# Second MLP of a two-block layer: h two tiles a strip, tables without GpSimd products, a bank for the row broadcast

## The chip, the cores and the metric

The kernel runs on one core of one Trainium2 chip, as one launch. The metric is the device time of a run in microseconds. A core has five engines with an instruction queue each: TensorE (PE, matrix products; its weight loads are shown as PEld), VectorE (DVE), ScalarE (ACT), GpSimd (POOL) and SyncE (SP), which here issues the weight transfers. An engine takes its queue in order. Products are written to eight banks of PSUM, from which VectorE and ScalarE read; everything else lies in SBUF.

## The reference, cut to what matters

The first block has two layers, each a mixer and then an MLP with modulated normalisation. The second block, which follows, has among other branches a state space one (S5).

```python
for l in range(2):
    ...                                            # mixer, x = x + g_m * rmsnorm(y)
    h = rmsnorm(x, norm_g[l, 2]) * (1.0 + sc_f) + sh_f
    y = jnp.square(jax.nn.relu(h @ w_up[l])) @ w_down[l]
    x = x + g_f * rmsnorm(y, norm_g[l, 3])
...                                                # second block: h @ w_in, then branches
```

There are 256 tokens, a width of 1024 and 4096 hidden units, all in fp32. The state space branch needs tables that depend on its parameters alone: powers 0 to 8 of a complex number lambda for 32 groups, times the input and output matrices B and C. As real numbers an entry is X1 times the real part plus X2 times the imaginary part: two products and one sum.

## The kernel before, in words

**Splitting.** Every fp32 weight and activation is written as a high part (fp32r) and the rest (low part), and a product is three matmuls: high by high, low by high, high by low. For each weight unit of 128 x 1024, ScalarE writes the high part (whi, line 379) and VectorE the rest (wlo, line 382). Three buffers each hold whi and wlo. The units stream in through SP into six buffers of two units.

**The MLP** (`mlp`, line 1283) walks over 32 strips of 128 hidden units. A strip is an up product (24 matmuls of 128x256) from h into a bank, then squared Relu, then a split into ml_h and ml_l (`act`), then an outer product with a unit of w_down (`kouter`, 24 matmuls) that adds into four banks `acc` of two output tiles each. `kouter` of strip j-1 is written behind `act` of strip j.

The first six strips don't wait for h. `begin` computes them from x and the modulation alone, with the scale per token (rs) still missing, into banks with the tags q, q, d, d, q, q. `act` of these strips reads the bank on VectorE with a product by rs (the tile ml_v), adds a column and applies Relu on ScalarE (ml_r), squares on VectorE (`stt`), and splits. The four banks of `acc` have the tag q as well, so they are those of the strips 0, 1, 4 and 5, each free when its strip's ml_v was read out.

**h** is made by `hprep(k, ...)` for eight tiles of 128 x 256: VectorE scales into a temporary t, ScalarE adds the shift into xh, VectorE writes the rest xl. All eight are written in the code behind strip 4, and t is a tile of the tag ml_v with two buffers, which `act` uses too. Strip 6 is the first that reads h.

**The tables** (`s5_prep`) are made during the second layer's MLP. It is a generator; the loop over strips advances it from strip 5 to strip 23 in proportion to the weights `_S5W` of its steps. It loads on ScalarE's queue, computes powers and angles in small VectorE steps, then nine table tiles WC (128 x 512: a VectorE product, a GpSimd product into s5tm, a VectorE sum) and 32 tiles WBs (128 x 128, the same three steps), which TensorE transposes in groups. GpSimd's queue also issues the transfers of the tables to memory and back (s5kd, s5TP).

**The end of the MLP** (`postnorm`, `plainsplit`): the four banks are squared and summed, the scale of each token is broadcast by TensorE into a bank (`rowsof`, tag o in a pool px of one bank), VectorE multiplies by it and adds to x in four steps (`xstep`), and x is split into xh, xl. Then the pool px closes and the pool pa opens with seven banks, and the branch's first product (`tokmajor`, 128x512, from xh and xl) is written there.

**Order.** The order of the instructions of each engine is not the one of the code: a planner goes through the program with estimated costs, and gives each free engine the ready instruction that stands first in the code. Only instructions inside `inorder` blocks keep the order of the code. The result is a fixed queue for each engine. Buffers and banks of one tag are given out in turn, with a wait for the last reader.

Of the kernel before, what the change touches and what calls it, by code (L numbers as in the profile page):

```python
# [28 lines left out]
AF = mybir.ActivationFunctionType  # L29
OP = mybir.AluOpType  # L30
# [4 lines left out]
P = 128  # L35
T = 256
# [6 lines left out]
_S5W = [0.1, 2, 1.5, 2.5, 2.5, 1.1, 2.6, 2.6, 1.5, 1.5, 1.1, 2, 2.5, 2.2] + [1.2] * 9 + [0.6] * 4 + \  # L43
# [268 lines left out]
class Prog:  # L312
# [967 lines left out]
        return self.postnorm(pool, xT, acc, l, 1, n, ("up", l, 1), ("up", l, 2))  # L1280


    def mlp(self, l, xT, pre, fill, n=0, up=None, yB=None):

        with self.pool(f"mlp{l}") as pool, self.psum(f"pf{l}", d=2, q=4, o=2):
            w = self.sb(up or pool, [P, 4608], "s5WC", F32R)[:, :16 * (T + 2)]
            w = w.rearrange("p (a k t) -> p a k t", a=2, k=8)
            ps, rs, hprep = self.begin(xT, pre, l, 2, (w[:, 0], w[:, 1]), pre[1],
                                       [("up", l, s) for s in range(6)], "qqddqq")
            del w  # L1290
            X = [self.sb(self.xp, [P, 8, T], k, F32R) for k in ("xh", "xl")]
            acc = None
            pend = []
            work = nst = 0

            def act(j):
                r = self.sb(pool, [P, T], "ml_r", bufs=2)
                if j < 6:
                    v = self.sb(pool, [P, T], "ml_v", bufs=2)
                    p, c = ps[j]  # L1300
                    self.tt(v, p[:, 0:T], rs, OP.mult)
                    self.act(r, v, AF.Relu, bias=c)
                    self.stt(r, v, c, r, OP.add, OP.mult)
                    ps[j] = p = None
                else:
                    p = self.strip(("up", l, j), X) if j < 31 else lastp
                    self.act(r, p, AF.Relu)
                    if l and j < 32:
                        self.act(r, r, AF.Square)
                    else:  # L1310
                        self.stt(r, p, 0.0, r, OP.max, OP.mult)
                hh = self.sb(pool, [P, T], "ml_h", F32R, 3)
                hl = self.sb(pool, [P, T], "ml_l", F32R, 3)
                self.hl(hh, hl, r)
                pend.append((hh, hl))

            raw = lambda j: self.unit(("down", l, j), 1024)
            for j in range(31):
                act(j)
                if j == 1:  # L1320
                    acc = [self.pt([P, 2, T], "q") for _ in range(4)]
                if j == 4:
                    for k in range(8):
                        hprep(k, X[0][:, k], X[1][:, k], self.sb(pool, [P, T], "ml_v", bufs=2))
                    del hprep
                    self.adasum()
                if j:
                    self.kouter(acc, raw(j - 1), *pend.pop(0), j == 1, False)

                while l and 5 <= j < 24 and work < sum(_S5W) * (j - 4) / 19 - 0.01:  # L1330
                    work += _S5W[nst]
                    nst += 1
                    next(fill, None)
                if not l:
                    next(fill, None)
            for _ in fill:
                assert False
            self.adasum()
            lastp = self.strip(("up", l, 31), X)
            W = self.split(raw(30), 1024)  # L1340
            W2 = self.split(raw(31), 1024)
            act(31)
            self.koutermm(acc, W, *pend.pop(0), False, False)
            W = None
            if not l:
                self.presplit(("in", 1, "cq", 0))
                self.presplit2(("in", 1, "cq", 0))
            self.koutermm(acc, W2, *pend.pop(0), False, True)
            W2 = None
            X = None  # L1350
            if l:
                return self.postnorm(pool, xT, acc, l, 3, n, yB=yB())
            return self.postnorm(pool, xT, acc, l, 3, n, ("in", 1, "cq", 1), ("in", 1, "ckv", 0))
# [39 lines left out]
    def s5_prep(self, pool, sx, dp):  # L1393

        nc = self.nc
# [28 lines left out]
        Lr, Li = sb([P, 9, 32], "s5Lr"), sb([P, 9, 32], "s5Li")  # L1424
# [15 lines left out]
        f = lambda a: a.rearrange("p a b -> p (a b)")  # L1440
# [35 lines left out]
        bc = lambda a: a[:, :, None].to_broadcast([P, 32, 16])  # L1476
# [3 lines left out]
        X1, X2, tm = sb([P, 32, 16], "s5X1"), sb([P, 32, 16], "s5X2"), sb([P, 32, 16], "s5tm", bufs=2)  # L1480
# [5 lines left out]
        tm = sb([P, 32, 16], "s5tm", bufs=2)  # L1486
        self.tt(tm, C1, bc(ci), OP.mult)
        self.tt(X2, X2, tm, OP.subtract)
        B2 = v3(rb[:, 512:1024])
# [3 lines left out]
        for k in range(9):  # L1493
            w = WC[:, :, k]
            tm = sb([P, 32, 16], "s5tm", bufs=2)
            self.tt(w, X1, bc(Lr[:, k]), OP.mult)
            nc.gpsimd.tensor_tensor(tm, X2, bc(Li[:, k]), op=OP.mult)
            self.tt(w, w, tm, OP.add)
            yield

# [17 lines left out]
        for q in range(4):  # L1518
            gs = slice(8 * q, 8 * q + 8)
            b8 = lambda a: a[:, gs, None].to_broadcast([P, 8, 16])  # L1520
            WBs = sb([P, 8, 8, 16], "s5WBs")
            for s in range(8):
                w = WBs[:, :, s]
                tm = sb([P, 8, 16], "s5tm", bufs=2)
                self.tt(w, B1[:, gs], b8(Lr[:, s]), OP.mult)
                nc.gpsimd.tensor_tensor(tm, B2[:, gs], b8(Li[:, s]), op=OP.mult)
                self.tt(w, w, tm, OP.add)
                if s % 4 == 3:
                    yield
            for g in range(0, 8, 4):  # L1530
                ps = self.pt([P, 4, P], "o")
                for a in range(4):
                    self.tr(ps[:, a], WBs[:, g + a].rearrange("p s h -> p (s h)"))
                self.act(self.WB[:, 8 * q + g:8 * q + g + 4], ps)
                yield
# [971 lines left out]
    def run(self, out):  # L2507
        tc, nc, pool = self.tc, self.nc, self.pool
        with tc.tile_pool(name="dram", bufs=1, space=DRAM) as dp:
# [3 lines left out]
            with pool("ring") as self.ring, pool("wp") as self.wp:  # L2513
                xT = self.start1(c1.enter_context(pool("l01", "left")))
                c0 = ExitStack()
                self.l01b = c0.enter_context(pool("l01b", "left"))
                with pool("rp") as q:
                    self.rope(q)
                self.i8 = self.sb(self.l01b, [P, 8], "i8", F32R)
                self.act(self.i8, self.C("i8"))  # L2520
                for l in range(2):
                    self.mixconst(l)
                with self.psum("p0", d=2, o=1):
                    self.adas(1)
                    self.y0 = self.xsums(xT)
                    self.adas(1)
                    for k in (("cq", 0), ("cq", 1), ("ckv", 0)):
                        self.presplit(("in", 0) + k)
                pre = self.mixer(0, xT, [None, None, None], (1, 0, 1, 1), 1)
                pre = self.mlp(0, xT, pre, self.filler(2, 12), 1)  # L2530
                pre = self.mixer(1, xT, pre, (1, 0, 0, 1), 1)
                c0.close()
                with pool("s5t") as s5t:
                    with pool("s5x") as sx:
                        half = lambda: [self.sb(sx, [P, 4, T], k) for k in ("s5rb", "s5rc")]
                        pre = self.mlp(1, xT, pre, self.s5_prep(s5t, sx, dp), up=s5t, yB=half)
                        with self.psum("px", o=1):
                            X = self.plainsplit(xT, pre)
                    pre = self.y0 = None
                    xd = dp.tile([P, 8 * T], F32, name="xd")  # L2540
                    nc.gpsimd.dma_start(xd, xT.rearrange("p a b -> p (a b)"))
                    c1.close()
                    thp = c1.enter_context(pool("thp", "left"))
                    self.hgb = self.sb(thp, [P, 24], "hgb")
                    self.ts(self.hgb, self.col("gate_b"), 0.5, None, OP.mult)
                    self.th = [self.sb(thp, [P, 8, T], f"th{i}") for i in range(2)]
                    G = [self.sb(thp, [P, 4, T], k, F32R) for k in ("gh", "gl")]
                    with pool("s5") as p, self.psum("pa", d=3, x=4):
                        self.bg = chain(self.gates(X, 1), self.gates(X, 0, 0, 6))
                        self.s5(p, dp, X, G)  # L2550
                self.pos = -(-self.pos // CH) * CH
            self.nraw, self.nw = 3, 2
            with pool("ring") as self.ring, pool("wp") as self.wp:
# [106 lines left out]
```

## Time and profile before

| | |
|---|---|
| runs | 1461.97 us median of 3 (1461.76 to 1469.58) |
| profiled execution | 1464.17 us, its span 1462.4 us |
| mean granted TensorE clock | 0.979 of full |
| TensorE busy | 1369.8 us (94%) |
| VectorE busy | 868.5 us (59%) |
| ScalarE busy | 649.4 us (44%) |
| GpSimd busy | 81.4 us (6%) |
| moved by DMA | 311.71 MB, 213 GB/s in the mean |

Busy time counts an instruction from its start to its end; instructions of one engine overlap a little at their ends. "Idle before" and "waited for" name the instruction whose end let a waiting one go. The granted clock of TensorE has two levels, 1.0 (2.4 GHz) and half; a value between them is the mean over a stretch. In the trace the first layer's MLP lies at about 194 to 400 us and the second layer's at about 566 to 782; the first branch product comes at 790.

### The profile page before, as it was taken

The page shows a single profiled execution, that of the slowest core. Times are in us where ns is not written, and L with a number is a line of the kernel's source. Part 1 is how long each engine was busy: PE and PEld are TensorE (multiplying, and loading weights), DVE is VectorE, ACT ScalarE, POOL GpSimd, SP SyncE. Part 2 cuts the span into 40 slices and gives each one's busy share as a digit, 9 for nine tenths or more (in the row PEclk, how much of TensorE's full clock was granted, in tenths as well). Part 3 has the DMA queues.
Part 4 walks back from the last instruction along what each step waited for, and adds up shares of the span by engine and source line. Part 5 has one row for each costly group of instructions (what it writes and reads, how often), then busy time and mean ns, then how long its engine had stood idle before and what let it go on. Part 6 is the DMA issues. An engine that isn't in the chain of part 4 may idle for free. (4 is left out here: it accounts for less than half of the span.)

```text
span 1462.4 us, 26516 instructions
## 1 busy us (share of the span) xinstructions
PE 1369.8 (94%) x10795; PEld 1124.7 (77%) x10795; DVE 868.5 (59%) x1983; ACT 649.4 (44%) x1295; POOL 81.4 (6%) x128
## 2 busy tenths in 40 slices
PE   4999999999999999899998989999998999999996
PEld 1787788999988878898997978888987864445442
DVE  2776677555588667998565465567746663222224
ACT  2655555444556545564555444355242432121121
POOL 0000000000000010023220010000000013000001
PEclk9999999999999999999999999999999999999998
DMA  9735467665565247444783333232124969999980
GB/s 371 295 140 202 186 247 278 224 252 198 178 259 197 89 176 268 156 159 171 186 233 115 116 104 143 89 145 87 59 92 159 405 218 366 420 410 375 399 327 30
DMA packets 45999, 311.71 MB, mean 213 GB/s; under 512 B 5296, under 2 KB 5744, under 8 KB 9648
## 3 DMA queue, kind: packets, MB, share of 16 engines
q1 hardware_dynamic: 41264, 293.10, 52.9%
q0 software_dynamic: 3312, 13.50, 3.5%
q10 hardware_dynamic: 1296, 3.36, 0.6%
q8 instruction: 87, 1.43, 0.4%
q14 instruction: 40, 0.33, 0.1%
HBM read 306.46 MB, written 3.47 MB: 212 GB/s over the span
## 5 line engine op out<-in xcount | busy, mean ns | idle before, releaser
L382 DVE TENSOR_TENSOR wlo<-raw,whi 128x1024 fp32r<-128x1024 f32 (+3 forms) x292 | 332.2, 1141 | 196.2 <-ACT whi L379 190.7
L379 ACT ACTIVATE whi<-raw 128x1024 fp32r<-128x1024 f32 (+3 forms) x292 | 284.5, 978 | 282.4 <-PE ps_d L393 202.4
L393 PE MATMUL ps_d<-xh,whi 128*128 128x256 f32 (+1 forms) x1072 | 310.8, 291 | 1.6 <-ACT whi L379 0.9
L393 PE MATMUL ps_d<-xh,wlo 128*128 128x256 f32 x816 | 234.3, 287 | 3.7 <-DVE wlo L382 3.6
L393 PE MATMUL ps_d<-xl,whi 128*128 128x256 f32 x816 | 232.9, 285 | 0.0
L393 PEld LDWEIGHTS ps_d<-xh,whi 128*128 128x128 f32 x1072 | 207.3, 193 | 7.6 <-issue 2.7
L393 PEld LDWEIGHTS ps_d<-xh,wlo 128*128 128x128 f32 x816 | 155.9, 191 | 6.9 <-DVE wlo L382 5.1
L393 PEld LDWEIGHTS ps_d<-xl,whi 128*128 128x128 f32 x816 | 155.9, 191 | 1.5 <-issue 1.2
L393 PE MATMUL ps_q<-ml_l,whi 128*128 128x256 f32 x512 | 145.6, 285 | 5.3 <-DVE ml_l L382 5.2
L393 PE MATMUL ps_q<-ml_h,whi 128*128 128x256 f32 x512 | 144.5, 285 | 6.3 <-DVE s5thr L390 4.8
L393 PE MATMUL ps_q<-ml_h,wlo 128*128 128x256 f32 x512 | 144.9, 284 | 0.0
L393 PE MATMUL ps_d<-raw,xg 128*64 128x512 f32 x488 | 110.0, 595 | 1.3 <-DVE xg L387 1.3
L393 PEld LDWEIGHTS ps_q<-ml_h,whi 128*128 128x128 f32 x512 | 97.3, 191 | 7.6 <-issue 7.0
L393 PEld LDWEIGHTS ps_q<-ml_l,whi 128*128 128x128 f32 x512 | 97.8, 191 | 6.6 <-DVE ml_l L382 6.6
L393 PEld LDWEIGHTS ps_q<-ml_h,wlo 128*128 128x128 f32 x512 | 97.7, 191 | 0.0
L393 PEld LDWEIGHTS ps_d<-raw,xg 128*64 128x64 f32 x488 | 34.1, 137 | 68.9 <-issue 65.8
L390 DVE SCALAR_TENSOR_TENSOR ex_t<-ex_t,ps_d 128x256 f32<-128x256 f32 x16 | 6.7, 421 | 135.0 <-ACT ex_t L379 135.0
L393 PE MATMUL ps_d<-u,whi 128*128 128x258 f32 x256 | 75.8, 301 | 0.0
L393 PE MATMUL ps_d<-u,wlo 128*128 128x258 f32 x256 | 70.7, 295 | 0.3 <-DVE wlo L382 0.3
L393 PE MATMUL ps_d<-raw,cnd_s 128*32 128x256 f32 x768 | 53.9, 415 | 12.4 <-DVE cnd_s L386 10.5
L379 ACT ACTIVATE ex_t<-ps_d 128x256 f32<-128x256 f32 x16 | 6.1, 383 | 128.7 <-PE ps_d L393 128.7
L393 PE MATMUL ps_y<-raw,ex_hT 128*64 128x512 f32 x256 | 57.7, 592 | 0.0
(777 smaller groups left out, 2632.7 us busy)
## 6 DMA issues: line engine op xcount, KB each, us to landing
raw<-W SPq DMA_DIRECT2D x277, 1024.0 KB, 7.3
s5TP<-s5kd POOLq DMA_DIRECT2D x8, 256.0 KB, 10.6
th<-rows POOLq DMA_DIRECT2D x2, 1024.0 KB, 8.6
raw<-W SPq DMA_DIRECT2D x4, 512.0 KB, 10.2
xT<-xT ACTq DMA_DIRECT2D x1, 1024.0 KB, 20.2
xd<-xT POOLq DMA_DIRECT2D x1, 1024.0 KB, 4.8
th<-W POOLq DMA_DIRECT2D x1, 1024.0 KB, 5.0
xg<-W POOLq DMA_DIRECT2D x1, 1024.0 KB, 6.5
```

The costliest lines, as they stand in the source:

```text
L379: return self.pin(self.nc.scalar.activation(out, in_, f, bias=bias, scale=scale))
L382: return self.pin(self.nc.vector.tensor_tensor(out, a, b, op=op))
L390: return self.pin(self.nc.vector.scalar_tensor_tensor(out, a, s, b, op0=op0, op1=op1))
L393: i = self.nc.tensor.matmul(out, l, r, start=start, stop=stop, **k)
```

## The change

- `act` of the first six strips squares on ScalarE instead of VectorE (both layers).
- `hprep` is called for two tiles each behind the strips 1 to 4, instead of eight behind strip 4 (both layers). The temporaries are halves of a tile of 128 x 512 with two buffers: hp_t in the first layer, in the second the tiles s5X1 and s5X2 that the tables use later.
- The tables are advanced from strip 7 instead of 5, to the same end; the weights of the steps stay.
- The 9 + 32 GpSimd products of the tables are VectorE products.
- The pool px stays open until the state space branch is done, so the broadcast's bank isn't given out again; px and pa together hold eight banks.

```diff
-    def mlp(self, l, xT, pre, fill, n=0, up=None, yB=None):
+    def mlp(self, l, xT, pre, fill, n=0, up=None, yB=None, tmp=None):
...
                     self.act(r, v, AF.Relu, bias=c)
-                    self.stt(r, v, c, r, OP.add, OP.mult)
+                    self.act(r, r, AF.Square)
...
+                if 0 < j < 5:
+                    t = tmp(j) if tmp else self.sb(pool, [P, 512], "hp_t", bufs=2)
+                    for k in (2 * j - 2, 2 * j - 1):
+                        hprep(k, X[0][:, k], X[1][:, k], t[:, k % 2 * T:k % 2 * T + T])
+                    t = None
                 if j == 4:
-                    for k in range(8):
-                        hprep(k, X[0][:, k], X[1][:, k], self.sb(pool, [P, T], "ml_v", bufs=2))
                     del hprep
                     self.adasum()
...
-                while l and 5 <= j < 24 and work < sum(_S5W) * (j - 4) / 19 - 0.01:
+                while l and 7 <= j < 24 and work < sum(_S5W) * (j - 6) / 17 - 0.01:
...
             self.tt(w, X1, bc(Lr[:, k]), OP.mult)
-            nc.gpsimd.tensor_tensor(tm, X2, bc(Li[:, k]), op=OP.mult)
+            self.tt(tm, X2, bc(Li[:, k]), OP.mult)
             self.tt(w, w, tm, OP.add)
...
                 self.tt(w, B1[:, gs], b8(Lr[:, s]), OP.mult)
-                nc.gpsimd.tensor_tensor(tm, B2[:, gs], b8(Li[:, s]), op=OP.mult)
+                self.tt(tm, B2[:, gs], b8(Li[:, s]), OP.mult)
                 self.tt(w, w, tm, OP.add)
...
-                        pre = self.mlp(1, xT, pre, self.s5_prep(s5t, sx, dp), up=s5t, yB=half)
-                        with self.psum("px", o=1):
-                            X = self.plainsplit(xT, pre)
+                        pre = self.mlp(1, xT, pre, self.s5_prep(s5t, sx, dp), up=s5t, yB=half,
+                                       tmp=lambda j: self.sb(sx, [P, 32, 16], f"s5X{1 + j % 2}").rearrange("p a b -> p (a b)"))
+                        c3 = ExitStack()
+                        c3.enter_context(self.psum("px", o=1))
+                        X = self.plainsplit(xT, pre)
...
                     with pool("s5") as p, self.psum("pa", d=3, x=4):
                         self.bg = chain(self.gates(X, 1), self.gates(X, 0, 0, 6))
                         self.s5(p, dp, X, G)
+                    c3.close()
```

## Rows read from the trace of the kernel before

**Rows 1.** Stages: PE, PEld, DVE, ACT, POOL busy us (instructions), clock, DMA, GB/s.

```profile
592.00:606.00 14.00, 9.24 (x69) 9.07 (x68) 14.00 (x62) 6.99 (x16) 0.00 (x0) 0.89 0.21 76
606.00:640.00 34.00, 33.90 (x284) 33.69 (x284) 34.00 (x76) 23.38 (x35) 0.00 (x0) 0.99 0.53 179
640.00:684.00 44.00, 38.70 (x303) 37.48 (x302) 42.26 (x56) 20.27 (x34) 23.25 (x19) 0.96 0.41 145
684.00:777.00 93.00, 91.90 (x822) 90.72 (x821) 54.53 (x101) 54.01 (x88) 17.35 (x34) 1.00 0.72 201
777.00:790.00 13.00, 6.74 (x48) 5.80 (x46) 9.75 (x28) 8.38 (x20) 0.00 (x0) 0.90 0.24 83
```

**Rows 2.** Waits of TensorE, 592 to 800 us: total, times, longest.

```profile
PE ps_d L393 <- DVE s5rc L382: 5.9, 1, 5.9
PE ps_q L393 <- DVE s5thr L390: 4.8, 1, 4.8
PE ps_q L393 <- DVE ml_l L382: 4.7, 3, 2.0
PE ps_o L401 <- DVE s5WBs L382: 1.1, 1, 1.1
...
PE ps_d L393 <- DVE wlo L382: 0.6, 1, 0.6
```

**Rows 3.** Waits of TensorE, 226 to 245 us.

```profile
PE ps_q L393 <- DVE ml_v L382: 1.5, 1, 1.5
PE ps_q L393 <- DVE ml_l L382: 0.6, 1, 0.6
```

**Rows 4.** Waits of TensorE, 800 us to the end: the largest.

```profile
PE ps_d L393 <- ACT gl_t L379: 4.5, 4, 1.5
```

**Rows 5.** Timeline of VectorE, 587 to 604 us: start, us, instruction.

```profile
588.37 0.19 DVE L1471 COPY s5swap<-c 128x64 f32<-128x64 f32 x1
...
588.87 0.88 DVE L390 SCALAR_TENSOR_TENSOR ml_r<-ml_v,pn_c,ml_r 128x256 f32<-128x256 f32 x2
...
590.00 1.22 DVE L382 TENSOR_TENSOR wlo<-raw,whi 128x1024 fp32r<-128x1024 f32 x1
...
602.54 0.48 DVE L390 SCALAR_TENSOR_TENSOR ml_v<-xT,pn_A,pn_r 128x256 f32<-128x256 f32 x1
602.93 0.41 DVE L382 TENSOR_TENSOR ml_v<-ps_q,pn_r 128x256 f32<-128x256 f32 x1
```

**Rows 6.** Timeline of TensorE: the first outer product of the second MLP.

```profile
592.15 0.28 PE L393 MATMUL ps_q<-ml_h,whi 128*128 128x256 f32 x1
```

**Rows 7.** Groups by form, GpSimd, 645-684 us: busy, mean ns | idle before.

```profile
L1497 POOL TENSOR_TENSOR s5tm<-s5X,s5Li 128x512 f32<-128x512 f32 x9 | 15.7, 1754 | 106.6 <-ACT whi L379 98.7 <-DVE s5WC L382 7.9
```

**Rows 8.** Groups by form, VectorE, 645 to 684 us.

```profile
L382 DVE TENSOR_TENSOR wlo<-raw,whi 128x1024 fp32r<-128x1024 f32 x11 | 16.1, 1468 | 0.0
L382 DVE TENSOR_TENSOR s5WC<-s5X,s5Lr 128x512 f32<-128x512 f32 x9 | 8.5, 969 | 0.0
...
L382 DVE TENSOR_TENSOR s5X<-s5X,s5tm 128x512 f32<-128x512 f32 x1 | 0.7, 686 | 0.0
```

**Rows 9.** Timeline of VectorE at 645 us, two table products.

```profile
645.30 1.29 DVE L382 TENSOR_TENSOR s5WC<-s5X,s5Lr 128x512 f32<-128x512 f32 x2
```

**Rows 10.** Timeline of VectorE at 732 us, eight small products.

```profile
732.74 1.70 DVE L382 TENSOR_TENSOR s5WBs<-s5rb,s5Lr 128x128 f32<-128x128 f32 x8
```

**Rows 11.** Timeline of all engines, 786 to 796 us.

```profile
786.65 1.33 ACT L379 ACTIVATE xh<-xT 128x256 fp32r<-128x256 f32 x4 [3.18 <-DVE xT L382]
...
789.64 0.68 DVE L382 TENSOR_TENSOR s5rc<-s5rc,ps_o 128x512 f32<-128x512 f32 x1
...
790.47 0.76 PE L393 MATMUL ps_d<-whi,xh 128*128 128x512 f32 x1 [5.87 <-DVE s5rc L382]
...
791.51 1.22 DVE L382 TENSOR_TENSOR wlo<-raw,whi 128x1024 fp32r<-128x1024 f32 x1
...
795.23 0.39 PE L393 MATMUL ps_d<-wlo,xh 128*128 128x512 f32 x1
```

## The prediction

> **What bounds the kernel now.** I read the table by stage first, then the list of what TensorE waits for, then the timelines around each wait. In the second block's MLP VectorE sets TensorE's waits. From 592 to 606 us VectorE is busy 14.00 of 14 us and TensorE 9.24; from 640 to 684 it is 42.26 of 44, and there GpSimd is busy 23.25 [rows 1]. TensorE's longest waits between 592 and 800 us are 5.9, 4.8, 4.7 (three), 1.1 and 0.6 us, and VectorE ends every one of these [rows 2]. In the first block's MLP there are two, 1.5 and 0.6 us [rows 3]. After 800 us the largest group of waits is 4.5 us in four pieces, and no row of that view names a transfer [rows 4]: from there on the order is TensorE's, so time won before it should arrive at the end. The waits have a second price: the granted clock is 0.89, 0.96 and 0.90 in three of the stretches [rows 1], that is, part of each ran at the lower of the two levels (1.2 instead of 2.4 GHz).
>
> **The change part by part.** The sum is made against the profiled execution, 1464.2 us, which is 2.2 above the median of the runs.
>
> *The h tiles (both MLPs).* The down product needs four banks that four of the first six outputs held. The last comes free when VectorE has read the sixth output, at 602.93; that read stands behind all eight h tiles, the last begun at 602.54 [rows 5], because reads and h tiles share a ring of two buffers (ml_v). TensorE waits 4.8 us for it [rows 2]. Afterwards h tiles have buffers of their own and come two a strip, so the read needs only a buffer that the fourth output's Relu gives back early. From both sides: in strict program order the read stays behind the h tiles and gains only the squares that leave VectorE (two take 0.88 us [rows 5], 0.4 each in sequence, five ahead of the read: 2.0 us); and if the first two h tiles (four instructions of 0.39 us, the distance from 602.54 to 602.93) go ahead of the weight split of 590.00 [rows 5], TensorE starts 1.6 us later: a gain of 0.4. At the other end the whole wait goes, 4.8 us, and with it the low clock of that stretch, 14 x 0.11 = 1.5 us. VectorE's own need decides between them. An instruction starts some 0.09 us before the end of the one ahead (602.54 + 0.48 against 602.93), so a read or an ml_l of 0.41 counts 0.33, a split of 1.22 counts 1.13. After the two reads that are done at 588.37 [rows 5], four reads, six ml_l, sixteen h instructions and six splits are 1.3 + 2.0 + 6.2 + 6.8 = 16.3 us, until 604.7. The outer products begin at 592.15 [rows 6], and the five ahead of the first strip that needs all of h are 120 matmuls at 34 us / 284 = 0.12 us [rows 1], 14.4 us, until 606.5. So it fits with 1.8 us over, which the state space steps that the plan slips in between use up. I count 4.8 + 1.2 of clock - 1.5 left = 4.5 us. The squares moved to ScalarE cost nothing: it is busy 6.99 of these 14 us [rows 1]. If that cover went, each would add 0.4 us to the chain of one strip.
>
> In the first block the two waits (2.1 us [rows 3]) lie behind the same chain, without state space steps. Between 0 and 2.1 I take 1.9, near the upper end since the squares alone give back 2.0.
>
> *The products without GpSimd.* Nine large products of 1.75 us on GpSimd [rows 7] become VectorE ones at 0.60 (1.29 us for a pair, 0.69 for one [rows 8, 9]), 32 small ones become 0.20 each (1.70 for eight [rows 10]): 5.4 + 6.4 = 11.8 us more VectorE work. What it gives back: while GpSimd ran, the weight split took 1468 ns in the mean [rows 8] against 1.22 us before [rows 5], eleven of them 2.7 us; nine table products took 969 against 686 for the same shape [rows 8], 2.5 us. With the shorter groups around them I estimate 7 us back between 645 and 684, where nine large and about eight small products cost 7.0. So where TensorE waits VectorE has no more to do than now, and its instructions are no longer late by a neighbour that the plan did not count. The other small products fall where VectorE is busy 54.53 of 93 us [rows 1]. TensorE's waits here are 4.7 + 0.6 + 1.1 us [rows 2], and 44 x 0.04 = 1.8 us of clock [rows 1], of which I count 1.5: 7.9. Bounds: 0 (VectorE just as late) and 8.2; below nothing is the third rival. I leave 2.0 for waits that a longer saturated stretch makes; not more, since from 606 to 640, before GpSimd began, VectorE was busy 34.00 of 34 us and TensorE still 33.90 [rows 1]. Gain 5.9 us.
>
> The Trainium skill (SBUF — State Buffer, Who interferes with whom) says that a VectorE instruction with two SBUF inputs and a GpSimd one that reads SBUF exclude each other, the second waiting until the first is done. By it up to the whole of each large product, nine of 1.75 us or 15.8, would be lost on VectorE; the rows show some 7, so the trace has only part of it. By the rule VectorE would come out of the stretch early, nothing of the 2.0 us would be left, and the sum would be 2 us more.
>
> *The later start of the tables* (strip 7 for 5, same end at 23). The plan takes ready steps early whatever their place: the swap table's copy ran at 588.37, among the first six outputs [rows 5]. I count nothing beyond the 2.0 left above. Queues: the order of weight loads on SP doesn't change; GpSimd's queue keeps its transfers and loses the products ahead of them, so they can only be earlier; the two table loads are on ScalarE's queue.
>
> *The bank of the row broadcast.* TensorE's first product after the MLP begins at 790.47, right behind the last read of the broadcast (789.64 + 0.68), though its first input is written by 787.0 (four in 1.33 us from 786.65) [rows 11]. With a bank of its own the broadcast holds nothing back: up to 3.4 us. Next late is the second weight split, 791.51 + 1.22 = 792.7; the first product that reads it is the 14th and now runs at 795.23 [rows 11]. Thirteen steps at today's mean of 0.37 us from 787.1 end at 791.9, so it would wait for the split: 2.4 us. Bounds: 0, if another wait ends at 790.4 as well, and 3.4 + 13 x 0.10 of clock [rows 1] = 4.7. I take 2.4 and leave the clock as it is: the gap shrinks from 5.9 to 2.5 us, and the three waits of 4.7 us (longest 2.0 [rows 2]) had a stretch of lower clock with them too.
>
> Sum: 1.9 + 4.5 + 5.9 + 2.4 = 14.7 us. 1464.2 - 14.7 = 1449.5; against the median, 1447.
>
> **The rivals.**
> *Everything goes (0.14).* No wait is left in the MLPs, the boundary's clock comes back: 2.1 + 6.3 + 8.2 + 4.7 = 21.3 us, 1441. For it: the 1.8 us of room for the h tiles. Against: VectorE's stretch without idle time gets longer.
>
> *VectorE stays late (0.25).* The sixth read keeps its place behind h (0.4 to 2.0 us, take 1), and half the waits of the tables come back as waits for weight splits: 1.9 + 1 + 3 + 2.4 = 8.3 us, 1453.7. For it: VectorE is full from 592 to 684 [rows 1], and only the squares and the GpSimd delay are taken from it. Against: the saturated 34 us with hardly a wait.
>
> *VectorE overflows, and the time ends higher (0.06).* The table steps keep their weights in the plan although a step now has three VectorE products instead of two, and are spread over 17 strips instead of 19. If place in the program outweighs readiness, 11.8 us and the room of two strips (48 matmuls, 5.8 us, less 2.6 of VectorE's own: 3.2 each) push weight splits back by 18 us, with three more clock stretches of 1.5, and the first split moves by 1.6: 24.1, less 1.9, 2.4 and the 7.9 of today's waits, is 11.9 us more, 1474. It decides from the point where the backlog passes the splits that TensorE has ahead. The Trainium skill (Perfetto Trace Analysis, Optimizing Scalar/DVE Operations) leans this way: with VectorE saturated, work may go to ScalarE or even GpSimd. It adds that between these two it might not help, as they share a port; the slower splits [rows 8] agree with that.
>
> *It doesn't do what it says (0.06).* The read still lands late and another bank holds the first product back: 2 to 3 us, 1459.5.
>
> **How the numbers follow.** The forecast has the remaining 0.49, with a range of its own from 1443 to 1452. A measurement of this kernel tells 0.5%, or 7.3 us, from no change: below 1454.7 counts as faster. Forecast, first rival and 0.15 of the second give 0.78; 0.10 of the second and the last 0.16; the overflow 0.06. The range from 1439 to 1458 leaves out the overflow and the last rival, and ends 2 us below the first.
>
> **What would show it.** Right: no wait for an output's read or an h tile near 598 us and clock 1.00 there; no weight split in VectorE above 1.3 us from 640 to 690 and no products on GpSimd; the first 512-column product close behind its first input, with a wait for the second split behind it. Wrong: TensorE waits for wlo or ml_l between 690 and 720 that are not there now, a late start of the first outer product, or a broadcast read that still ends the wait at the boundary.

## The result: 22 us faster, and the profile after

The changed kernel took 1441.5 us (median of 4 runs, 1438.4 to 1446.7) beside 1463.8 for the kernel before on the same chip: ratio 0.9847, 95% interval 0.9825 to 0.9869, or 19 to 26 us less. The forecast was 1447 and faster, with 1443 to 1452 as its own range and 1439 to 1458 in all: the median lies 1.5 us below the first and inside the second. Its profiled execution took 1441.92 us (span 1440.1) at a mean granted clock of 0.980, against 1464.17 (1462.4) at 0.979.

The same stages as in [rows 1], each moved by what the changed kernel is ahead there (5.8 us at the start of the second MLP; columns as there):

```profile
586.00:600.00 14.00, 13.28 (x105) 12.48 (x104) 13.68 (x31) 11.40 (x24) 0.00 (x0) 1.00 0.27 86
600.00:634.00 34.00, 33.30 (x281) 33.09 (x281) 33.99 (x101) 21.42 (x32) 0.00 (x0) 1.00 0.52 189
634.00:678.00 44.00, 44.00 (x374) 44.00 (x373) 44.00 (x79) 25.46 (x40) 0.00 (x0) 1.00 0.50 187
678.00:759.00 81.00, 79.93 (x719) 78.71 (x719) 51.82 (x119) 46.54 (x78) 7.88 (x12) 1.00 0.74 202
759.00:770.00 11.00, 8.33 (x49) 6.97 (x47) 6.16 (x20) 6.59 (x14) 0.00 (x0) 0.84 0.27 98
```

In the first row TensorE does 13.28 us of work in 14 where it did 9.24, and ScalarE, which now has the squares too, 11.40 for 6.99. In the third VectorE is busy for 44.00 of 44 us, fuller than before, and TensorE for 44.00 too: a saturated VectorE holds nothing up as long as its work is done in time. The 12 instructions that GpSimd has left in the fourth row are its transfers. TensorE's waits from 586 to 780 us (total, times, longest), which answer to [rows 2]:

```profile
PE ps_d L393 <- ACT xh L379: 2.5, 1, 2.5
PE ps_o L401 <- DVE s5WBs L382: 0.9, 1, 0.9
PE ps_o L393 <- ACT xh L379: 0.9, 1, 0.9
PE ps_q L393 <- DVE ml_l L382: 0.7, 1, 0.7
PE ps_q L393 <- DVE wlo L382: 0.5, 1, 0.5
```

Of the waits of 4.8 us (for the sixth read) and 4.7 us (for ml_l) the first is gone and 0.7 us is left of the second; the 5.9 us at the boundary are 2.5 and end with another releaser. The 0.9 us for xh, at the boundary too, stood in the kernel before as well, in the line that [rows 2] leaves out: not every wait there ended with VectorE. In the first MLP, 223 to 245 us, one wait is left of the two in [rows 3]; after 780 us the largest is the one of [rows 4], unchanged:

```profile
PE ps_q L393 <- DVE ml_v L382: 0.2, 1, 0.2
```

```profile
PE ps_d L393 <- ACT gl_t L379: 4.5, 4, 1.5
```

VectorE by form, 625 to 680 us, beside [rows 8] (busy, mean ns | idle before). Nothing is stretched any more; the split is back at 1222 ns from 1468, the table product at 689 from 969:

```profile
L382 DVE TENSOR_TENSOR wlo<-raw,whi 128x1024 fp32r<-128x1024 f32 x20 | 24.4, 1222 | 0.0
L382 DVE TENSOR_TENSOR s5WC<-s5X,s5Lr 128x512 f32<-128x512 f32 x9 | 6.2, 689 | 0.0
L382 DVE TENSOR_TENSOR s5tm<-s5X,s5Li 128x512 f32<-128x512 f32 x9 | 6.2, 689 | 0.0
```

The sixth read in the changed kernel, beside [rows 5]: it still comes directly behind the eighth h tile, but that pair stands at 592 us, and the read begins 6.4 us behind the first outer product (586.38) instead of 10.8. VectorE's timeline (start, us):

```profile
592.34 0.48 DVE L390 SCALAR_TENSOR_TENSOR s5X<-xT,pn_A,pn_r 128x256 f32<-128x256 f32 x1
592.73 0.41 DVE L382 TENSOR_TENSOR ml_v<-ps_q,pn_r 128x256 f32<-128x256 f32 x1
```

### The profile page after: what moved, and what is told of

It is laid out like the page before. It is cut to its first block, busy times and chain, and to the rows that moved or that the text cites. A ratio compares the mean times of both kernels' runs of the same rounds, so it can differ in the third digit from the quotient of the medians.

```text
span 1440.1 us, 26492 instructions
## 1 busy us (share of the span) xinstructions
PE 1360.6 (94%) x10795; PEld 1117.6 (78%) x10795; DVE 864.5 (60%) x2012; ACT 651.9 (45%) x1307; POOL 48.5 (3%) x87
```

## The experiments

Twelve kernels were run, in three sets of four, each set beside its own runs of the kernel before (the third, with squares alone, no fillers, early tables and GpSimd behind the tables, on another chip than the first two). Each run's ratio is against the kernel before. The table has, from one profiled execution each, the length of the three places of the change: the first and the second MLP from first to last outer product, the boundary from there to the first branch product; then the rest of the span, and the end of the sixth read behind the first outer product in the second MLP.

| kernel | median us | ratio, interval | MLP 1 | MLP 2 | boundary | rest | sixth read |
|---|---|---|---|---|---|---|---|
| before | 1463.8 to 1465.9 | | 171.7 | 187.1 | 11.2 | 1092.4 | 11.2 |
| changed | 1441.5 | 0.9847 (0.9825-0.9869) | 169.4 | 175.0 | 9.3 | 1086.4 | 6.8 |
| changed again | 1443.6 | 0.9843 (0.9819-0.9867) | 169.4 | 175.0 | 8.4 | 1093.8 | 6.8 |
| h alone | 1455.9 | 0.9924 (0.9903-0.9945) | 169.4 | 182.0 | 12.7 | 1089.4 | 6.8 |
| products alone | 1457.1 | 0.9932 (0.9913-0.9950) | 171.7 | 178.9 | 12.2 | 1091.9 | 11.2 |
| bank alone | 1460.2 | 0.9949 (0.9930-0.9968) | 171.7 | 187.1 | 7.9 | 1091.0 | 11.2 |
| eight h, own buffers | 1442.5 | 0.9848 (0.9827-0.9869) | 168.9 | 173.7 | 7.9 | 1090.2 | 1.0 |
| two h, shared ring | 1449.3 | 0.9893 (0.9865-0.9921) | 169.8 | 176.5 | 7.9 | 1093.2 | 9.3 |
| squares alone | 1462.2 | 0.9979 (0.9965-0.9992) | 171.2 | 185.6 | 12.5 | 1094.2 | 9.9 |
| squares undone | 1452.9 | 0.9926 (0.9901-0.9951) | 170.8 | 177.6 | 9.3 | 1092.5 | 9.1 |
| early tables | 1441.6 | 0.9860 (0.9833-0.9887) | 169.4 | 173.8 | 7.9 | 1085.2 | 6.8 |
| eight h, no fillers | 1443.9 | 0.9865 (0.9842-0.9888) | 168.9 | 173.8 | 8.1 | 1089.3 | 1.0 |
| GpSimd beside tables | 1448.7 | 0.9902 (0.9880-0.9924) | 169.4 | 178.9 | 8.9 | 1088.1 | 6.8 |
| GpSimd behind tables | 1456.7 | 0.9938 (0.9917-0.9959) | 169.4 | 187.3 | 9.3 | 1091.5 | 6.8 |

The rest is the part that no edit touches. It goes from 1085.2 to 1094.2 us, in two profiled executions of the one changed kernel 1086.4 and 1093.8. The two MLPs repeat to 0.1 us in these two; the boundary doesn't.

### The three parts alone, and all again

The edits are the three parts of the diff above: the h tiles with the squares; the GpSimd products; the pool px.

> The kernel before with the h tiles alone changed: two a strip, temporaries of their own, the squares of the first six strips on ScalarE. My theory of the prediction gives 1.9 us in the first MLP and 4.5 us in the second: 6.4 us faster, and the two kernels' traces say how the 16.3 us at the places of the change split. Read from the changed kernel's trace, the first MLP alone gave 2.3 us (227.43 to 398.87 us before, 225.45 to 394.62 after). If the sixth output's read is the only thing that h sets, the second MLP gives 4.8 us and the sum is 7 us. Rival: the products on GpSimd still stretch VectorE behind it, so that part of the 4.8 us is lost again in waits for ml_l between 650 and 690 us; then 3 to 5 us in all. A second rival is on the 6 us that lie outside the change's places (2.0 us ahead of 204 us, 1.5 us in the mixer, 2.6 us behind the boundary): if they are due to the lower clock's stretches falling elsewhere by chance, this kernel's times of those stretches scatter too and follow no edit.

> The kernel before with the 9 + 32 GpSimd products of the tables on VectorE and nothing else. My theory: 5.9 us faster (7.9 us of waits and clock go, 2.0 us of new waits come), and no weight split above 1.3 us on VectorE. In the changed kernel the second MLP is 12.1 us shorter; less the 4.8 us of the sixth read this leaves 7.3 us for the products, so 6 to 8 us if the parts add. Rival, VectorE overflows: with h and the squares as they were, the 11.8 us of products come on top of a full VectorE and the result is 0 to 4 us only, with waits for wlo or ml_l between 640 and 700 us.

> The kernel before with the bank of the row broadcast kept to the end of the state space branch, nothing else. My theory: 2.4 us faster, the first product of the branch then starts right behind its first input (3.4 us earlier), and a later one waits for the second weight split that ends at 792.7 us. Rival: the clock of the boundary comes back as well and it gives 3.4 to 4.7 us. Other rival: the gap keeps its length because the postnorm's filler products or the broadcast are in the way, 0 to 1 us.

> The changed kernel once more, on the same chip and against the same runs of the kernel before. First measured: 22.4 us faster (0.9847, 0.9825 to 0.9869). The places of the change give 16.3 us by the two traces (2.3 in the first MLP, 12.1 in the second, 1.9 at the boundary). If the 6 us elsewhere are scatter of where the lower clock falls, this run gives 16 to 22 us and its trace has its lower-clock stretches in other places outside the change; if they belong to the change, the same 2.0, 1.5 and 2.6 us are there again. The three parts alone should add up to this run's gain, if nothing is shared between them; a sum that is smaller by more than 2 us says that two of the parts need each other.

Measured at the places: h gives 2.3 us in the first MLP and 5.1 in the second, the products 8.2, the bank 3.4. All together give 2.3 + 12.1, and 1.9 and 2.8 at the boundary in the changed kernel's two executions, where the clock was lower than with the bank alone (0.82 and 0.75 against 1.00). So about 1 us of the second MLP is shared between h and the products, the rest adds up by place. By the medians of the runs the three gains add up to 24.5 us and the whole is 22.3. TensorE's waits in the second MLP show that h and the products cure two different things. With h alone, 580 to 800 us, the sixth read is no longer in the list, but the splits behind GpSimd are:

```profile
PE ps_q L393 <- DVE ml_l L382: 3.6, 5, 1.2
PE ps_d L393 <- DVE wlo L382: 2.2, 3, 1.4
```

With the products alone it is the other way round, and no wait for ml_l is left:

```profile
PE ps_q L393 <- DVE s5thr L390: 4.7, 1, 4.7
...
PE ps_d L393 <- DVE wlo L382: 0.2, 1, 0.2
```

The 4.7 us are put down to s5thr, a small table step, since it came last by the profile; the run with h alone shows that the wait was the sixth read's. The overflow rival of the products is out: 8.2 us is above the top of what it allowed.

The run of all again shows the lower clock in other places: in the mixer before the second MLP (176.0 us in place of 171.7) and in the stretch behind the first branch product (70.3 in place of 67.1), while the places of the change kept their lengths. The 6 us of the first pair that lie outside are therefore not shown to be of the change, but scatter of single executions. What the clock alone does is seen in the stretch from the last outer product of the first MLP to the first of the second: 191.5 us in each of the six executions that had the full clock there, and in the other eight 193.0 us (at 0.99) to 198.9 (at 0.96). The time ahead of the first MLP doesn't follow the clock like that (227.4 us at 0.98 before, 225.5 at 0.95 changed), so the clock isn't all of the scatter.

### Whether the ring or the place made the read late

The changed kernel, with eight h tiles written behind strip 4 that keep temporaries of their own:

```diff
-                if 0 < j < 5:
-                    t = tmp(j) if tmp else self.sb(pool, [P, 512], "hp_t", bufs=2)
-                    for k in (2 * j - 2, 2 * j - 1):
+                if j == 4:
+                    for k in range(8):
+                        if k % 2 == 0:
+                            t = tmp(k // 2 + 1) if tmp else self.sb(pool, [P, 512], "hp_t", bufs=2)
```

and with two h tiles a strip that take their temporaries from the shared ring:

```diff
-                        hprep(k, X[0][:, k], X[1][:, k], t[:, k % 2 * T:k % 2 * T + T])
+                        hprep(k, X[0][:, k], X[1][:, k], self.sb(pool, [P, T], "ml_v", bufs=2))
```

> The changed kernel with the h tiles put back together: all eight are written behind strip 4, but keep temporaries of their own and the squares stay on ScalarE. It asks whether the place of the h tiles or the ring of buffers they shared made the sixth read late. My theory (the ring): about the changed kernel's time, 0 to 1 us slower, and no wait of TensorE for the sixth read above 1 us, since the planner may take a ready h tile whatever its place. Rival (the place): the reads are again behind h, TensorE waits 2 to 5 us near 592 us, and the kernel is 3 to 6 us slower than the changed one (the second MLP 178 to 180 us long from its first to its last outer product, against 175.0).

> The changed kernel with the h tiles two a strip, but with temporaries from the ring of two buffers that the reads use (the tag ml_v, as before). If the ring is what made the read late, the second MLP is 177 to 180 us from first to last outer product, against 175.0 of the changed kernel and 182.0 of the run with h alone, and the first 170.5 to 171.7 against 169.4; the kernel is 3 to 6 us slower than the changed one. Rival: two tiles a strip by themselves put the read early enough, and the time is the changed kernel's within 1 us.

In the second MLP it was the ring. Written behind strip 4 with buffers of their own, the h tiles don't hold the reads back: the fifth and sixth stand together at 587.25 (first outer product 587.00), ahead of the last four h tiles, and TensorE waits for none of them. Both MLPs are shorter than in the changed kernel, by 0.5 and 1.3 us. VectorE, that kernel and then the one with the shared ring, whose sixth read begins 8.9 us behind its first outer product (590.83):

```profile
587.25 0.75 DVE L382 TENSOR_TENSOR ml_v<-ps_q,pn_r 128x256 f32<-128x256 f32 x2
```

```profile
599.73 0.41 DVE L382 TENSOR_TENSOR ml_v<-ps_q,pn_r 128x256 f32<-128x256 f32 x1
```

The kernel with the shared ring missed its expectation: its MLPs are 0.4 and 1.5 us longer than the changed kernel's, not 1.1 to 2.3 and 2 to 5. So the place does something too, where the ring is shared. The first MLP shows how much, since nothing but h and the squares differs there: with the squares on ScalarE it takes 171.2 us with eight tiles in the shared ring (the kernel with squares alone, below), 169.8 with two a strip in that ring, 169.4 with two a strip in buffers of their own and 168.9 with eight in their own. The place alone is worth 1.4 us there and the buffers alone 2.2; they cure the same wait. With own buffers two a strip is the slower place by 0.5 and 1.3 us; there h tiles of earlier strips stand ahead of the reads.

### The squares

Undone in the changed kernel (and, the other way round, made alone in the kernel before):

```diff
-                    self.act(r, r, AF.Square)
+                    self.stt(r, v, c, r, OP.add, OP.mult)
```

> The changed kernel with the squares of the first six strips back on VectorE. My prediction put 2.0 us of the first outputs' chain on them (0.4 us each, five ahead of the sixth read). In the first MLP, where nothing else differs, the theory gives 1.5 to 2.1 us longer than 169.4 us if the squares make that gain, and 0 to 0.3 if the order of the h tiles makes it. In the second MLP VectorE has the room of 1.8 us less: 1 to 2 us longer than 175.0. Rival: h starts so early that the squares cost nothing, both MLPs keep their lengths within 0.3 us.

> The kernel before with the squares of the first six strips on ScalarE, and the h tiles left as they were (eight behind strip 4, in the ring of two). My prediction's bound for this case, the read keeping its place behind h, was a gain of 2.0 us (five squares of 0.4 us). Taking the squares out of the changed kernel cost 1.4 us in the first MLP and 2.6 in the second. If the squares do the same here, the first MLP is 170.2 us from first to last outer product (171.7 before, 169.4 changed) and the second 184.5 (187.1 before); 3 to 5 us faster in all. Rival (the ring holds the reads back whatever VectorE has to do): 0 to 0.5 us in the first MLP, 0 to 1 in the second.

Undone in the changed kernel they cost 1.4 and 2.6 us; done alone in the kernel before they gain only 0.5 and 1.5, and the sixth read (602.05) still stands behind the last h tile. The expectation that they do the same in both missed, and the second MLP also gained more than the rival's 0 to 1 us. In the kernel before the read moves by 1.3 us (its end from 11.2 to 9.9), in the changed one by 2.3 (6.8 to 9.1), on either side of the 2.0 us that five squares of 0.4 make. With the squares back, TensorE waits for splits, 583 to 778 us:

```profile
PE ps_q L393 <- DVE wlo L382: 2.8, 2, 2.5
```

### GpSimd's products beside and behind the tables

Two kernels, one addition each to the changed one:

```diff
             self.tt(tm, X2, bc(Li[:, k]), OP.mult)
+            nc.gpsimd.tensor_tensor(self.WB[:, 4 * (k % 8):4 * (k % 8) + 4].rearrange("p g (h a) -> p (g h) a", a=16), X2, bc(Li[:, k]), op=OP.mult)
...
             if s % 2:
+                for _ in range(4):
+                    nc.gpsimd.tensor_tensor(X1, X2, bc(Li[:, 1]), op=OP.mult)
                 yield
```

> The changed kernel with nine GpSimd products added beside the nine large ones of VectorE: same two inputs, 128x512, result into a part of the table that is written over later and that nothing waits for early. VectorE's own work is the changed kernel's, so only the neighbour is added. My theory (the neighbour stretches VectorE): the weight splits between 640 and 690 us take 1.4 to 1.6 us in the mean again where a GpSimd product runs (1.22 without), 5 to 8 us of VectorE time are lost, waits for ml_l or wlo come back and the second MLP is 3 to 8 us longer than 175.0. Rival (what the products cost before was the order, with VectorE's sums waiting for GpSimd's result): the splits stay at 1.22 us and the second MLP at 175 within 1 us.

> The changed kernel with sixteen GpSimd products added behind the tables, four after every second table transfer, of the same shape and inputs as the large table products (128x512); nothing reads their result. There VectorE is not full (68 us of 97 between 660 and 757), so that GpSimd gets its turn. When VectorE ran back to back, a GpSimd product begun at 645.51 ended only 38.46 us later and the splits stayed at 1.22 us; behind it, where VectorE had pauses, splits took 2.08, 1.27 and 1.64 and GpSimd's products 1.05 to 2.04. Theory (the two exclude each other, and who comes second waits): splits that meet a product here take 1.3 to 2.1 us, ten or more of them, VectorE loses 5 to 12 us, and as VectorE has 29 us to spare here TensorE loses under 1.5 us. Rival (the slower splits before had another cause, the load on SBUF of all engines together): splits stay within 1.3 us and the products at 1.05.

Neither went as expected. In the first, GpSimd's work (start, us) was shut out:

```profile
645.51 49.75 POOL L1501 TENSOR_TENSOR s5WB<-s5X,s5Li 128x512 f32<-128x512 f32 x9 [100.95 <-DVE s5X L382]
```

Of these 49.75 us the first product has 38.46, the others 1.05 to 2.04. VectorE ran without a pause from 645.5 us and kept its durations, up to the split of 682.96. Its timeline around the end of the first product, at 683.97:

```profile
681.28 1.22 DVE L382 TENSOR_TENSOR wlo<-raw,whi 128x1024 fp32r<-128x1024 f32 x1
682.42 0.41 DVE L382 TENSOR_TENSOR ml_l<-ml_r,ml_h 128x256 fp32r<-128x256 f32 x1
682.76 0.28 DVE L382 TENSOR_TENSOR s5tm<-s5rb,s5Li 128x128 f32<-128x128 f32 x1
682.96 2.08 DVE L382 TENSOR_TENSOR wlo<-raw,whi 128x1024 fp32r<-128x1024 f32 x1
...
690.17 4.10 DVE L390 SCALAR_TENSOR_TENSOR s5ks<-c,colt,s5ks 128x16 f32<-128x16 f32 x4
```

Four tiny sums of 128x16 take 4.10 us beside GpSimd's products, one product's length each. The eight sums of this kind by tile (durations in ns, min/median/max), first in the changed kernel, then here:

```profile
L390 DVE SCALAR_TENSOR_TENSOR s5ks<-c,colt,s5ks x8: 228/229/235, 685.2 to 691.6; 128x16 f32<-128x16 f32 x8
```

```profile
L390 DVE SCALAR_TENSOR_TENSOR s5ks<-c,colt,s5ks x8: 230/632/1103, 690.2 to 700.2; 128x16 f32<-128x16 f32 x8
```

So the two do exclude each other, whole instruction against whole instruction: 0.23 us of work waits 0.8 more for a product in progress, and a product waits 37 us for a VectorE that never pauses. The rule of the Trainium skill (SBUF — State Buffer, Who interferes with whom) that the one who comes second is blocked until the other's instruction has ended agrees with the sums. It does not give the 37 us: many VectorE instructions ended meanwhile, and none of their ends let the product in. The turn came at the split of 682.96, whose high part ScalarE had written at 682.92, 0.04 us before; for every earlier split and ml_l of that stretch the input had been ready for 0.29 us or more. The second kernel repeats it: its first product, begun at 667.88, ends 14.11 us later, 1.0 us into a split of 2.08 us (680.99) whose high part was ready at 680.95. So a row of VectorE instructions whose inputs lie ready kept GpSimd out for all its length. That a gap too short for the timeline let it in is the likely reading of the 0.04 us, but no row shows such a gap.

What it cost came by another way than expected. The table's transfer to memory stands behind the products in GpSimd's queue; ScalarE's copy into s5ks waits for it, a bank of tag o for that copy, and TensorE for the bank: 2.9 of the 3.9 us by which the second MLP is longer. In the second kernel the planner put all sixteen products ahead of that transfer, and this chain alone costs 10.7 us of the 12.3. GpSimd there, then TensorE (the last bracket is the wait and its releaser):

```profile
667.88 33.82 POOL L1545 TENSOR_TENSOR s5X<-s5X,s5Li 128x512 f32<-128x512 f32 x16 [124.13 <-DVE s5WC L382]
701.64 1.49 POOL L1517 DMA_DIRECT2D s5kd<-s5ks  x2
```

```profile
704.44 0.47 PE L401 MATMUL ps_o<-c,s5WBs 128*128 128x128 f32 x1 [10.72 <-ACT s5ks L379]
```

For the question it was made for, splits that meet a product where VectorE has room, the second kernel says little: TensorE stood still meanwhile, and only three splits met one (2.08, 1.27, 1.63 us). Its places give only 4.0 us against the kernel before and its median 8.3; the profiled execution was the slowest of its six, and the difference stays open.

### The later start of the tables, and the fillers at the boundary

The fillers are TensorE products whose result nothing reads (`hold`: four there, eight matmuls), written ahead of the last row broadcast. The first edit is made in the changed kernel, the second in the one with eight h tiles and own temporaries:

```diff
-                while l and 7 <= j < 24 and work < sum(_S5W) * (j - 6) / 17 - 0.01:
+                while l and 5 <= j < 24 and work < sum(_S5W) * (j - 4) / 19 - 0.01:
...
-        self.hold(self.C("ones"), sq[:, 1], 4)
+        if (l, j) != (1, 3):
+            self.hold(self.C("ones"), sq[:, 1], 4)
```

> The changed kernel with the tables advanced from strip 5 again instead of 7. My prediction counted nothing for the later start, because a ready step is taken early whatever its place. Theory: the second MLP is 175.0 us within 0.5 from first to last outer product. Rival (place outweighs readiness, early table steps stand ahead of splits): 1 to 3 us longer, with a wait for wlo or a read near 590 us.

> The kernel with all eight h tiles behind strip 4 and temporaries of their own, without the four filler products ahead of the last row broadcast. In the profiled run of the changed kernel these ran at the lower clock (8 matmuls in 3.46 us) and ended as the broadcast could have begun; where the clock stayed up the boundary took 7.86 us from the last outer product to the first branch product. Theory (the fillers are in the way): 0.5 to 1.5 us less at the boundary, and the kernel the fastest of all. Rival (they keep the clock up): the boundary is no shorter, a stretch of the lower clock of 6.8 us or more follows it, and the next stretch is 1.5 to 3 us longer (67.3 us from the first branch product to the first gate product).

The later start costs 1.2 us in the second MLP, where the forecast counted nothing and the expectation allowed 0.5: with the early start the wait of 0.7 us for ml_l is gone and the one of 0.9 for s5WBs is 0.4. The rival, early table steps that stand ahead of the splits, didn't show. Without the fillers the boundary took 8.1 us at a granted clock of 0.79. With them it took 7.9 in four kernels at clock 1.00, and 8.4 and 9.3 in the changed kernel at 0.75 and 0.82. So at the full clock they are not in the way, and the theory is out as a general cause. The rival's sign, a next stretch longer by 1.5 to 3 us, didn't show either (67.5 us beside 67.2 with fillers); whether the fillers keep the clock up can't be told from one execution. What they cost when they run at the lower clock is seen in the profiled execution of the changed kernel, all engines:

```profile
764.32 3.46 PE L393 MATMUL ps_d<-xh,c 128*128 128x256 f32 x8
...
766.07 0.28 DVE L390 SCALAR_TENSOR_TENSOR rs_y<-rs_t,rs_y 128x1 f32<-128x1 f32 x2
767.57 0.62 PE L401 MATMUL ps_o<-c,rs_y 128*128 128x128 f32 x2
...
770.70 0.50 PE L393 MATMUL ps_d<-whi,xh 128*128 128x512 f32 x1 [2.51 <-ACT xh L379]
```

The scale is ready at 766.35, the eight fillers (1.97 us at the full clock, 3.46 here) end at 767.78, and the broadcast behind them starts 1.2 us late. With the bank alone, at clock 1.0, the broadcast follows the scale at once and the first product again waits 2.5 us for xh alone:

```profile
788.79 0.28 DVE L390 SCALAR_TENSOR_TENSOR rs_y<-rs_t,rs_y 128x1 f32<-128x1 f32 x2
789.00 0.45 PE L401 MATMUL ps_o<-c,rs_y 128*128 128x128 f32 x2
...
791.96 0.50 PE L393 MATMUL ps_d<-whi,xh 128*128 128x512 f32 x1 [2.51 <-ACT xh L379]
```

No version is measurably faster than the changed one. The eight h tiles with own buffers and the early tables are 1.8 and 1.2 us shorter in the MLPs by the traces, less than the runs can tell.

## Why the prediction was right, point by point

**The direction and the places held.** VectorE set TensorE's waits; the three places of the change gave 16.3 us in the profiled pair (2.3 + 12.1 + 1.9), against 14.7 forecast, and would give 17.8 with the 3.4 that the bank alone gave at the full clock. Of the signs of being right one failed: no second split holds the branch products up. Of the signs of being wrong only a wait of 0.2 us for wlo at 706 us came.

**The h tiles (1.9 + 4.5 forecast).** 2.3 and, alone, 5.1 measured. The reason given first, the shared ring, is shown; two tiles a strip matter only where the ring is shared, and with own buffers eight at once did better. The way was not quite the forecast one: the read did not leave the h tiles behind, it still follows the eighth, only earlier. In the kernel before TensorE stood still from 598.7 us, 6.6 behind its first outer product; the read now begins at 6.4 and ends at 6.8, with waits of 0.7 us for splits ahead of it that put TensorE's need at some 7.3, so it is only just in time. My count of VectorE's need, which ended at 604.7, was 4.8 us too long: between the first two reads and the last xl the changed kernel has two splits, not six (four of 1.13 are 4.5), and three ml_l, not six. So there was more room than the 1.8 us I gave it.

**The products (5.9).** Mis-sized. Alone 8.2 us, on top of h 7.0 (182.0 - 175.0). The step that failed is the 2.0 us left for new waits of a longer saturated stretch: VectorE is full from 600 to 678 us, and TensorE's waits from the first to the last outer product come to 2.5 us. I had set the exclusion of the two engines aside because nine products of 1.75 us would be 15.8 and the rows showed 7 lost. But the 1.75 us held GpSimd's own waiting: with its turn a product takes 1.05 (nine are 9.5) and a small one 0.40 (ten are 4.0). VectorE's loss, which I put at 7, was 8.2 us of longer instructions by form against the changed kernel's means (split, table product, table sum, ml_l, small product and small sum) and 1.3 us of waiting for GpSimd's results, of which the table sums have 1.0 (VectorE by form, kernel before, 645 to 684 us):

```profile
L382 DVE TENSOR_TENSOR s5WC<-s5WC,s5tm 128x512 f32<-128x512 f32 x9 | 6.8, 775 | 1.0 <-POOL s5tm L1497 1.0
```

So the order, sums that wait for GpSimd, was the smaller part, and VectorE got some 9.5 us back for the 7.0 that I set against it. Read so, nothing of the 2.0 was to be left, and the sum would have been 16.7. That agrees with the sum that I gave for the rule of the Trainium skill (same page and section).

**The bank (2.4).** Mis-sized, for a cause that isn't there. I let the 14th product wait for the split at 791.51 and so gave back 1.0 of 3.4 us. With the bank alone the 14th product runs at 796.64, 12.55 us behind the last outer product (784.09) instead of 15.98, and the split that answers to the one at 791.51 begins at 796.36 and ends after it: it was not its input. The gain is the full 3.4 us. In the profiled pair it is 1.9, because the fillers met the lower clock; at the forecast's 2.4 two errors nearly cancelled.

**The later start (0).** It costs 1.2 us.

**The total.** The medians differ by 22.4 us, the places give 16.3 to 17.8. The rest of the span differed by 6.0 us in the first pair, and by -1.4 (1092.4 - 1093.8) in the second; over the 14 executions it scatters by 9 us. A least-squares fit to the 125 runs that list a clock, one level for each kernel and one common slope on the mean granted clock, gives 5.3 us for each 0.01 of clock (runs of both chips together). The 42 runs of before have 0.974 in the mean, the 9 of the changed kernel 0.979. At equal clock the changed kernel is 18.8 us ahead (plus or minus 1.9), near the sum of the places, and 3 us go with the clock; h, products and bank alone are 7.6, 6.8 and 4.3 ahead there (plus or minus 2), beside 7.4, 8.2 and 3.4 by place. For every kernel but the one with GpSimd behind the tables the sum of the three places and the gain at equal clock agree within 2.5 us. Part of the clock is the change's own, since its waits had lower clock with them (0.89 and 0.96 in [rows 1], 1.00 now). Whether the higher clock outside the places belongs to the change stays open: one execution of a kernel is profiled, and those seen don't follow the edits. So the gain is above the forecast because the places gave 1.6 to 3.1 us more than the sum, and some 3 us go with a clock that the sum did not have; what is left is within the scatter.

**The rivals.** The first, all waits gone at 1441, has the measured time by luck: 2.5 us of waits are left in the second MLP and 2.5 for xh at the boundary, the places give 16.3 to 17.8 us and not its 21.3, and the rest came from elsewhere. VectorE late, overflow and no effect are out. Of the rule of the Trainium skill beside overflow (Perfetto Trace Analysis, Optimizing Scalar/DVE Operations) the part on ScalarE is borne out by the squares (1.4 and 2.6 us when undone); for GpSimd the doubt that the page adds is.

## What to carry to other kernels

Before you move instructions because a read comes late, look at who shares its ring of buffers: temporaries of their own did more than a new place in the program (2.2 against 1.4 us in the first MLP). Here a GpSimd product beside a VectorE near saturation cost its whole length to one of the two, so read GpSimd's busy time as waiting first, and see what is queued behind it. When a change's places give less than the runs, compare the stretches that it doesn't touch over several executions before you explain them.

## What the runs showed of the hardware

A GpSimd product of two SBUF inputs begun at 645.51 us ended 38.46 us later, while VectorE ran instructions of two SBUF inputs back to back, and it got its turn at the first split whose input came only 0.04 us ahead; with VectorE pausing, the same product took 1.05 us and stretched a 0.23 us sum to 1.1. And the lower clock cost the boundary 1.5 us (9.3 against 7.9), not by slower products alone but because filler products at half rate held back a short one that the next stage waited for: without fillers it took 8.1 us at a clock of 0.79.
